# The first load of Q as two DMAs: 16 partitions and 112

## The chip, the cores and the metric

The kernel runs on one core of a Trainium2 chip. The metric is device microseconds of one execution, taken as the median of several runs. A profile is one more execution, recorded by the hardware profiler; it has a time of its own, and a span, which goes from the first to the last recorded instruction. A core has five instruction streams: PE (TensorE, matrix products; its weight loads are listed as PEld), DVE (VectorE), ACT (ScalarE), POOL (GpSimd) and SP (SyncE, which here only issues DMAs). Sixteen DMA engines move data between HBM and the core's on-chip memory, which has 128 partitions.

## What is computed

Linear attention over 8 batches of 12 heads, 512 positions of 64 features, all float32:

```python
Q_feat = np.maximum(0, Q) + 1
K_feat = np.maximum(0, K) + 1
KV = np.einsum('bhkd,bhkv->bhdv', K_feat, V)
K_sum = np.sum(K_feat, axis=2)
numerator = np.einsum('bhqd,bhdv->bhqv', Q_feat, KV)
denominator = np.einsum('bhqd,bhd->bhq', Q_feat, K_sum)
return (numerator / (denominator[:, :, :, None] + 1e-10)).astype(np.float32)
```

Each of Q, K, V and the output is 12.58 MB, so 50.33 MB pass between HBM and the core.

## The kernel before

The work is cut into 12 groups of 8 heads, and loads and stores cover 1 MB of the on-chip side as a rule. For a group g the stages are: `k_features` (DVE, K + 1 against 1, to bfloat16), `v_blocks` (V copied into a block layout, three quarters by DVE and one by ACT), `q_features` (DVE), `keys_values` (PE, the sums over positions, with ACT copying the result out), `transposes` (PE, with ACT copying), `out_matmuls` (PE) and `norms` (DVE, reciprocal and multiply). The main loop runs over the groups, with the output two groups behind and the stores three behind (`LAG`); the last two groups are written out by hand. The order on each engine is the order of the program.

Nearly all loads go through POOL's queue (`nc.gpsimd.dma_start`), which turns float32 in HBM into bfloat16 on the chip as it moves. They are `load` (line 115, K and V), `load_rest_q` (line 98) and `load_q` (line 121). Most stores go through POOL's queue too (line 135); those of the last two groups go through SP's (lines 138 and 141).

One load is different. `load_first_q` brings the first 128 x 2048 numbers of Q, one row of 8 KB for each partition, through SP's queue, and leaves them in float32 (line 93). It is the first thing that SP does. Beside it POOL issues, in this order: K and V of group 0, the second 128 rows of Q, K and V of group 1, and after some constants the loads of groups 2 and 3. The rows of `q_first` are read by DVE in `q_features` of groups 0 and 1 (line 146), after the features of K and the copies of V of group 0.

Of the kernel before, what the change touches and what calls it, by code (L numbers as in the profile page):

```python
# [19 lines left out]
def kernel(  # L20
# [19 lines left out]
    nc = tc.nc  # L40

    B, H, S, D = Q.shape
    P = 128
# [10 lines left out]
    def view(t, c):  # L54
        return t.flatten_outer_dims().rearrange("(n p c) d -> p n c d", p=P, c=c)

    q_eights = view(Q, C4)
# [32 lines left out]

    def load_first_q():
        t = head_pool.tile([P, C4, D], FP32, name="q_first")
        nc.sync.dma_start(out=t, in_=q_eights[:, 0])
        return t

    def load_rest_q(t):
# [159 lines left out]
    with tc.manual_schedule():  # L256
        nc.gpsimd.memset(zero, 0.0)
        q_first = load_first_q()
        load("k", (0,))
        load("v", (0,))  # L260
# [81 lines left out]
```

## Time and profile before

| | us |
|---|---|
| three runs, median (lowest to highest) | 126.62 (126.32 to 127.39) |
| the profiled execution | 126.47 |
| its span | 124.7 |
| DVE busy (share of the span) | 90.1 (72%) |
| PE busy | 64.2 (52%) |
| ACT busy | 59.6 (48%) |
| POOL busy | 26.1 (21%) |
| the first load of Q: issue to landing | 4.9 |
| the first loads of K and V: issue to landing | 7.0 and 8.7 |
| DVE's first read of the first load of Q starts at | 12.95 |

Times are counted from the start of the span. "L93" is line 93 of the kernel. A DMA is a set of packets, each handled by one of the sixteen DMA engines; a row of 8 KB of the first load is one packet. Queue q1 is SP's, q0 is POOL's, and q8 and q14 bring instructions. In a stretch of the span, the DMA share is the time of the packets that start in it, divided by sixteen engines and the stretch's length, so it can exceed 1 in a short stretch; GB/s counts bytes as they land, so a load that turns float32 into bfloat16 counts half of what it reads.

### The profile page before, as it was taken

What the parts mean: (1) busy time and instruction counts of PE and PEld (TensorE: products, weight loads), DVE (VectorE), ACT (ScalarE), POOL (GpSimd) and SP (SyncE); (2) the same over time, 40 slices, a digit from 0 to 9 for tenths busy, and PEclk for the clock granted to TensorE, in tenths of its full rate; (3) what the DMA queues carried; (4) which work ended last, traced back from release to release, by engine and by line L of the source; (5) the groups of instructions that cost most, each with busy time, mean ns of one, the idle gap of its engine ahead of it and who ended that gap; (6) DMA issues with size and microseconds to landing.
All of it is one profiled execution on the core that took longest, in us unless ns stands there. A gap on an engine that the chain in (4) does not pass through costs nothing.

```text
span 124.7 us, 2349 instructions
## 1 busy us (share of the span) xinstructions
PE 64.2 (52%) x960; PEld 52.6 (42%) x960; DVE 90.1 (72%) x190; ACT 59.6 (48%) x86; POOL 26.1 (21%) x53
## 2 busy tenths in 40 slices
PE   0000874600596837939099690069394369874200
PEld 0000654600475826829088490058183158663000
DVE  4875735206999989998999950799958799969700
ACT  7505169806009981398803981603982283650000
POOL 6992020400001460207202070302020200020000
PEclk9999999995559996799855999657999855999655
DMA  3999999999999999999999999999999999999993
GB/s 89 320 212 216 206 211 212 212 215 218 206 212 212 220 213 206 212 215 217 230 406 327 210 212 219 212 342 395 230 202 215 219 247 417 419 417 415 406 409 135
DMA packets 11819, 32.13 MB, mean 258 GB/s; under 512 B 544, under 2 KB 544, under 8 KB 11680
## 3 DMA queue, kind: packets, MB, share of 16 engines
q0 software_dynamic: 10592, 28.84, 97.5%
q1 hardware_dynamic: 1216, 3.15, 6.7%
q8 instruction: 7, 0.11, 0.3%
q14 instruction: 4, 0.03, 0.1%
HBM read 37.75 MB, written 12.58 MB: 404 GB/s over the span
## 4 chain that ended last, share of the span: by engine, by line
DMA 51%; DVE 19%; PE 10%; ACT 7%; POOL 6%; issue 2%; DVEq 0%; ACTq 0%; POOLq 0%
DMA v_raw<-in_V_dram 51%; DVE o_sb L232 7%; PE kva_ps L180 7%; DVE v_all L164 7%; ACT qt L204 3%; ACT v_all L162 3%; POOL kva_all L271 2%; POOL k_raw L115 2%; DVE recip L231 2%; PE qt_ps L201 1%; PE o_ps L214 1%; POOL v_raw L115 1%; DVE qf L146 1%; DVE qt L204 1%; DVE kf L146 1%
## 5 line engine op out<-in xcount | busy, mean ns | idle before, releaser
L180 PE MATMUL kva_ps<-v_all,kf 128*64 128x260 bf16 x384 | 33.0, 343 | 16.8 <-DVE v_all L164 15.5
L214 PE MATMUL o_ps<-kva_all,qt 128*64 128x130 bf16 x384 | 19.7, 237 | 34.2 <-DVE recip L231 25.9
L164 DVE COPY v_all<-v_raw 32x2048 bf16<-32x2048 bf16 x36 | 26.1, 725 | 15.0 <-DMA v_raw<-in_V_dram 14.6
L180 PEld LDWEIGHTS <-kf 128*64 128x64 bf16 x384 | 26.6, 140 | 20.4 <-DVE v_all L164 15.9
L232 DVE TENSOR_TENSOR o_sb<-o_ps,recip 128x512 f32<-128x512 f32 x48 | 33.2, 692 | 1.6
L162 ACT COPY v_all<-v_raw 32x2048 bf16<-32x2048 bf16 x12 | 22.6, 1893 | 18.2 <-DMA v_raw<-in_V_dram 18.0
L214 PEld LDWEIGHTS <-qt 128*64 128x64 bf16 x384 | 13.7, 116 | 39.1 <-issue 23.2
L190 ACT CAST kva_all<-kva_ps 64x256 bf16<-64x256 f32 x24 | 8.9, 370 | 30.7 <-PE kva_ps L180 30.6
L204 ACT COPY qt<-qt_ps 128x1024 bf16<-128x1024 bf16 x23 | 22.2, 1015 | 2.2 <-PE qt_ps L201 1.7
L201 PE MATMUL qt_ps<-identity,qf 128*128 128x128 bf16 x192 | 14.8, 236 | 1.3 <-ACT qt L204 1.1
L135 POOL DMA_DIRECT2D out_dram<-o_sb x10 | 8.3, 830 | 32.1 <-DVE o_sb L232 27.3
L146 DVE TENSOR_SCALAR kf<-k_raw 128x1024 bf16<-128x1024 bf16 x24 | 9.5, 436 | 7.0 <-DMA k_raw<-in_K_dram 7.0
L201 PEld LDWEIGHTS <-qf 128*128 128x128 bf16 x192 | 12.6, 107 | 4.1 <-issue 1.8
L115 POOL DMA_DIRECT2D k_raw<-in_K_dram x7 | 5.4, 765 | 34.4 <-DVE kf L146 34.0
L231 DVE RECIPROCAL recip<-o_ps 128x8 f32<-128x8 f32 x48 | 9.6, 200 | 1.5 <-PE o_ps L214 1.2
L115 POOL DMA_DIRECT2D v_raw<-in_V_dram x7 | 5.4, 772 | 17.4 <-ACT v_all L162 17.4
L146 DVE TENSOR_SCALAR qf<-q_raw 128x1024 bf16<-128x1024 bf16 x22 | 8.2, 432 | 0.0
L249 DVE MEMSET v_all<- 128x2600 f32 x2 | 4.5, 2225 | 1.1 <-issue 1.1
L191 ACT CAST kva_all<-kva_ps 64x4 bf16<-64x4 f32 x24 | 4.1, 169 | 0.0
L121 POOL DMA_DIRECT2D q_raw<-in_Q_dram x5 | 3.5, 705 | 0.0
L250 ACT COPY v_all<-zero 128x1560 f32<-128x1560 f32 x2 | 2.9, 1488 | 0.0
L271 POOL MEMSET kva_all<- 128x130 bf16 x16 | 2.4, 196 | 0.0
(14 smaller groups left out, 6.6 us busy)
## 6 DMA issues: line engine op xcount, KB each, us to landing
out_dram<-o_sb POOLq DMA_DIRECT2D x10, 1024.0 KB, 25.2
k_raw<-in_K_dram POOLq DMA_DIRECT2D x5, 1024.0 KB, 21.7
v_raw<-in_V_dram POOLq DMA_DIRECT2D x5, 1024.0 KB, 21.8
q_raw<-in_Q_dram POOLq DMA_DIRECT2D x5, 1024.0 KB, 25.9
q_first<-in_Q_dram SPq DMA_DIRECT2D x1, 1024.0 KB, 4.9
k_raw<-in_K_dram POOLq DMA_DIRECT2D x2, 512.0 KB, 9.7
v_raw<-in_V_dram POOLq DMA_DIRECT2D x2, 512.0 KB, 11.4
out_dram<-o_sb SPq DMA_DIRECT2D x1, 1024.0 KB, 7.0
```

The lines of the kernel that those rows point to most:

```text
L115: nc.gpsimd.dma_start(out=bufs[x, s][:, ms], in_=drams[x][:, of])
L135: nc.gpsimd.dma_start(out=o_to[:, g % 2 : 2 * NP : 2], in_=outs[s][:, g % 2 : 2 * NP : 2])
L146: nc.vector.tensor_scalar(out=dst, in0=src, scalar1=1.0, scalar2=1.0, op0=ALU.add, op1=ALU.max)
L162: nc.scalar.copy(out=v_all[ps, g % 2, :, :, b * D : b * D + D], in_=v_raw[ps])
L164: nc.vector.tensor_copy(out=v_all[ps, g % 2, :, :, b * D : b * D + D], in_=v_raw[ps])
L180: nc.tensor.matmul(kva_ps[64 * n : 64 * n + 64], lhsT=kf[:, c, n, :], rhs=v_all[:, g % 2, n, c, :], start=(c == 0), stop=(c == C2 - 1),)
L190: nc.scalar.copy(out=kva[ps, :, n, 0:D], in_=kva_ps[ps, 0 : 4 * D].rearrange("p (b d) -> p b d", b=4))
L201: nc.tensor.transpose(qt_ps[:, c, r], qf[:, r, 2 * half + c, :, :], identity)
L204: copy(out=qts[g // 2][:, lo : lo + 2], in_=qt_ps.rearrange("p c r q -> p c q r"))
L214: nc.tensor.matmul(ops[c // 4][64 * j : 64 * j + 64, c // 2 % 2, (c % 2) * W : (c % 2) * W + W], lhsT=qt[:, c, q : q + 16, :], rhs=kva[:, ...
L231: nc.vector.reciprocal(out=recip, in_=cells[:, :, :, :, D:D1])
L232: nc.vector.tensor_tensor(out=o_sb[:, 2 * h + g % 2 : 2 * NP : NP, 4 * i : 4 * i + 4].rearrange("p n (b c) d -> p b c n d", b=2), in0=cell ...
```

## The change

The one DMA of `load_first_q` becomes two of the same queue: the first brings partitions 0 to 15, the second partitions 16 to 127. The tile, its place and its later reads stay. DVE's first read of it now waits for both.

```diff
     def load_first_q():
         t = head_pool.tile([P, C4, D], FP32, name="q_first")
-        nc.sync.dma_start(out=t, in_=q_eights[:, 0])
+        nc.sync.dma_start(out=t[0:16], in_=q_eights[0:16, 0])
+        nc.sync.dma_start(out=t[16:P], in_=q_eights[16:P, 0])
         return t
```

On the engines the instructions keep their order; SP has one DMA more, ahead of its stores. Lines below 93 stand one lower in the changed kernel.

## The prediction

> **What bounds the kernel now.** I read the page's slices first, then its DMA queues, then stretches of the span at the start and the end, then the critical chain's place for SP's first load.
>
> The slices of the span (DMA is the mean busy share of 16 DMA engines in tenths) and the queue shares:
>
> ```profile
> DMA  3999999999999999999999999999999999999993
> ...
> q0 software_dynamic: 10592, 28.84, 97.5%
> q1 hardware_dynamic: 1216, 3.15, 6.7%
> q8 instruction: 7, 0.11, 0.3%
> ...
> HBM read 37.75 MB, written 12.58 MB: 404 GB/s over the span
> ```
>
> The DMA engines are full in every slice but the first and the last, while the busiest compute engine, DVE, works 72% of the span. So the time is: when the stream starts, plus bytes over rate, plus what follows the last byte. The change touches only the start. Busy times by stretch (columns: window, length, five engines' busy time with counts, TensorE clock, DMA share, GB/s):
>
> ```profile
> 1.00:1.70 0.70, 0.00 (x0) 0.00 (x0) 0.18 (x3) 0.70 (x1) 0.41 (x1) 1.00 0.00 0
> 1.70:1.90 0.20, 0.00 (x0) 0.00 (x0) 0.03 (x1) 0.20 (x1) 0.20 (x1) 1.00 2.84 328
> 1.90:2.50 0.60, 0.00 (x0) 0.00 (x0) 0.60 (x1) 0.59 (x2) 0.60 (x2) 1.00 0.00 0
> 2.50:2.90 0.40, 0.00 (x0) 0.00 (x0) 0.40 (x1) 0.40 (x1) 0.40 (x2) 1.00 0.51 205
> 2.90:4.90 2.00, 0.00 (x0) 0.00 (x0) 1.41 (x3) 2.00 (x2) 2.00 (x4) 1.00 1.04 434
> ...
> 121.80:123.50 1.70, 0.00 (x0) 0.00 (x0) 0.00 (x0) 0.00 (x0) 0.00 (x0) 0.50 0.51 195
> 123.50:124.70 1.20, 0.00 (x0) 0.00 (x0) 0.00 (x0) 0.00 (x0) 0.00 (x0) 0.50 0.00 0
> ```
>
> A packet counts in the stretch where it starts, with its whole duration. From 1.70 to 1.90 us start 328 GB/s x 0.2 us = 65.6 KB, that is 8 packets of 8 KB (one row of Q each); they take 2.84 x 16 x 0.2 / 8 = 1.14 us apiece. Then nothing starts for 0.6 us. From 2.50 on, 10 packets start in 0.4 us and take 0.51 x 16 x 0.4 / 10 = 0.33 us apiece, and from 2.90 on 434 x 2.0 / 8.192 = 106 packets, 0.31 us apiece. So eight of the sixteen engines begin at about 1.75 us with one slow packet, the other eight only at about 2.55, and both groups are in full stream by 2.9 to 3.1. At the end the engines stop one after the other between 121.8 and about 123.4: a share of 0.51 over 1.7 us is 0.87 us of work on the mean engine, so the mean engine ends near 122.7, and the last one, which sets the time, some 0.7 us later.
>
> What SP issues (start, duration, instruction):
>
> ```profile
> 0.74 0.39 SPq L93 DMA_DIRECT2D q_first<-in_Q_dram  x1
> 114.28 0.39 SPq L138 DMA_DIRECT2D out_dram<-o_sb  x1
> 115.96 2.05 SPq L141 DMA_DIRECT2D out_dram<-o_sb  x2
> ```
>
> **The change, part by part.** The profiled execution took 126.47 us, its span 124.7, so 1.77 us lie around the span; the sum is made against 126.47, which is 0.15 below the median 126.62 (126.32 to 127.39).
>
> *One issue more on SP.* One more L93 instruction, 0.39 us by its row. Behind it on SP stands only the store of L138, which goes out at 114.28, so the issue itself costs nothing. What it delays is the 112 rows: their issue runs from 1.13 to 1.52 instead of from 0.74. POOL's queue is not moved: its first K load is issued at 1.29 as before. DVE's first feature of Q now waits for two DMAs in place of one; it runs at 12.95, and Q landed at 0.74 + 4.9 = 5.6 us, 7.3 us of cover for DVE, for the queue behind that wait (the other features of Q, then K's and V's of group 1) and for TensorE's transposes. Without that cover the price would be the 0.39 us.
>
> *The start of the engines.* If the sixteen rows reach all sixteen engines at 1.75 and each streams at 0.31 us a packet from there, the late eight gain 2.55 - 1.75 = 0.8 us and the early eight lose their slow packet's excess, 1.14 - 0.31 = 0.83: a gain of 0.8 at most. The other end is no gain: the early eight hold a 0.8 us lead and have it eaten by the slow packet (1.75 + 1.14 = 2.89), while the late eight's first packets are over at 2.55 + 0.33 = 2.88. Both rows say that bytes begin to arrive at one moment, near 2.6 us, whoever asked first. I take -0.1: the nearest rows are these two, and they end together.
>
> *A second start.* At worst the 112 rows pay a slow first packet of their own: +0.83. But the late eight started 0.8 us after the early ones and their first packets took 0.33, so slowness belongs to the first request of all and not to each one; and the second issue is over 1.4 us before those first packets end. Below nothing cannot be: a second start removes no byte. I take 0. If an engine did find nothing of Q in between, the first K load (issued from 1.29 to 2.13) is the work that hides it; without it the hole is the 0.39 us between the issues.
>
> *Two completions.* One more 4-byte packet on each engine; the Q stretch shows 144 packets on this queue for 128 rows, so 16 closing packets ride on the load today without a gap that shows in the 434 GB/s. At most they cost a whole small packet's slot; I take 0.01.
>
> *Other shares of the rows.* Today each engine carries 8 rows of 8 KB. Evenly cut, it carries 1 and 7, and nothing is added; which partitions one engine writes at a time changes, and no row shows the price. From below it could gain what the stretch from 2.90 leaves: 106 packets at 0.314 against 0.309, so 0.04 us on eight packets. From above, three rows too many on an engine (the slower rival) are 3 x 0.31 = +0.93. I take +0.1, near the even cut.
>
> Sum: 0 - 0.1 + 0 + 0.01 + 0.1 = about 0. Against 126.47 that is 126.5; carried to the median of the runs (+0.15) 126.65. I write 126.7.
>
> [...] For the end of the program the trace has two SP stores of 0.5 MB back to back, both 6.4 us to landing, in an unbroken stream of 407 GB/s from 116.0 to 121.8; cutting a transfer made no hole and no speed there. [...]
>
> **The rivals.**
>
> *Faster: the whole 0.8 us.* All sixteen engines stream from 1.75. For it: eight engines do sit idle from 1.75 to 2.55. Against it: the slow 1.14 us packets of those that did not. Time 126.62 - 0.8 = 125.8. To pass 1% it would need 0.4 us more, which only a change in how the engines end could give. Chance 0.16, of which 0.07 past 1%.
>
> *Slower: uneven shares.* If the rows are dealt in blocks by partition (that only eight engines had work at 1.75 fits blocks: the first half of the partitions to eight engines), sixteen rows may fall on four engines, four rows each, and the 112 are then cut evenly: 4 + 7 = 11 rows instead of 8 on those four, +0.93 us there and -0.31 elsewhere. It decides as soon as one of the four is an engine that ends within 0.9 us of the last one; as the mean engine ends only 0.7 before the last, one of four nearly surely does. Time from +0.2 to +0.93: 126.8 to 127.55. Against it: 128 rows came out even. Chance 0.24; to pass 1% it must meet another loss, such as two of the seven instruction loads (0.3% of 16 x 124.7 us, so about 0.9 us each, each on one engine) coming together on one engine that had one before; 0.12 of the 0.24, with a little more for losses that I can't name.
>
> *It does nothing.* The hardware hands on both loads as one list and eight engines still begin at 2.55: 126.6. Chance 0.1.
>
> **How the numbers follow.** Forecast 0.5, nothing 0.1, faster 0.16, slower 0.24. I take 1% (1.27 us) as what a measurement of this kernel can tell from no change; the three runs shown lie 0.85% apart. So past 1% faster (below 125.35) 0.08, past 1% slower (above 127.9) 0.15, within 0.77. The range: from 125.6 (the full 0.8 with the 0.2 to 0.3 by which the lowest run lies under the median) to 127.8 (the 0.93 with the same spread above); that leaves some 2 in 10 outside, most of it above.
>
> **What would show it.** Right: from 1.70 to 1.90 us sixteen packets of 8 KB start instead of eight, each slow (about 1.1 us); the stretch from 2.9 to 4.9 stays at about 430 GB/s; V's first copy stays near 10.8 us and the last packets near 123.4. Faster is right if packets that start before 2.0 take 0.3 us and Q is over at 4.3 instead of 5.1. Uneven shares are right if fewer than sixteen packets start near 1.75 and the engines' ends spread over more than 1.7 us. The forecast is wrong if a hole appears in the DMA slices between 3 and 5 us, or if any stage past 10 us moves by more than the stream's start did.

## The result, and the profile after

| | before | changed |
|---|---|---|
| median (lowest to highest), 22 runs each | 126.67 us (126.32 to 127.46) | 127.18 us (126.73 to 127.91) |
| ratio, 95% interval | | 1.0034 (1.0019 to 1.0048) |
| the profiled execution, its span | 126.47, 124.7 us | 127.62, 125.8 us |

The change costs 0.34%, which is 0.43 us (0.24 to 0.61): within 1%, inside the range, but not nothing. (The two medians lie 0.51 us apart, inside that interval.) Single executions of one kernel spread over more than 1 us, so the 1.1 us between the two profiled spans must not be read as the price; the interval over many runs is the price.

The slices and the queues of the changed kernel's page, to be held against those of before:

```profile
DMA  3999999999999999999999999999999999999992
...
q0 software_dynamic: 10592, 28.84, 96.7%
q1 hardware_dynamic: 1232, 3.15, 7.3%
q8 instruction: 7, 0.11, 0.3%
...
HBM read 37.75 MB, written 12.58 MB: 400 GB/s over the span
```

The DMA engines still have no pause: every slice but the first and the last reads 9. SP's queue q1 has 16 packets more (the second DMA's closing packets: the trace has 80 packets of 4 bytes on this queue instead of 64) and the same 3.15 MB, but its packets took 7.3% of the engines' span instead of 6.7%: the same bytes went more slowly. The stretches of the start show where (columns as before: window, length, busy times, clock, DMA share, GB/s):

```profile
1.70:1.90 0.20, 0.00 (x0) 0.00 (x0) 0.03 (x1) 0.20 (x1) 0.20 (x1) 1.00 0.00 0
1.90:2.20 0.30, 0.00 (x0) 0.00 (x0) 0.30 (x1) 0.29 (x2) 0.30 (x2) 1.00 1.12 437
2.20:2.50 0.30, 0.00 (x0) 0.00 (x0) 0.30 (x1) 0.30 (x1) 0.30 (x1) 1.00 2.47 328
2.50:2.90 0.40, 0.00 (x0) 0.00 (x0) 0.40 (x1) 0.40 (x1) 0.40 (x2) 1.00 0.00 0
2.90:3.50 0.60, 0.00 (x0) 0.00 (x0) 0.60 (x1) 0.60 (x2) 0.60 (x2) 1.00 0.66 232
3.50:4.90 1.40, 0.00 (x0) 0.00 (x0) 0.81 (x3) 1.40 (x2) 1.40 (x3) 1.00 1.04 328
4.90:5.30 0.40, 0.00 (x0) 0.00 (x0) 0.40 (x1) 0.01 (x1) 0.32 (x2) 1.00 1.08 307
```

Worked as in the prediction: from 1.90 to 2.20 start 437 x 0.3 / 8.192 = 16 packets of 8 KB, the sixteen rows, at 1.12 x 16 x 0.3 / 16 = 0.34 us apiece: sixteen at once, one for each engine by estimate, none of them slow. From 2.20 on the first packets of the 112 rows follow, 12 of them at 2.47 x 16 x 0.3 / 12 = 0.99 us. Then comes the difference that matters: from 3.50 to 4.90 56 packets take 1.04 x 16 x 1.4 / 56 = 0.42 us apiece, and 0.46 from 4.90 to 5.30, where before the packets from 2.9 to 4.9 took 0.31 on the mean. The engines' share is full (1.04 and 1.08); each packet takes a third to a half longer.

SP's issues and DVE's first work on the loads in the changed kernel (start, duration, instruction, in brackets the idle time before it):

```profile
0.74 0.39 SPq L93 DMA_DIRECT2D q_first<-in_Q_dram  x1
1.19 0.41 SPq L94 DMA_DIRECT2D q_first<-in_Q_dram  x1
```

```profile
9.02 0.83 DVE L147 TENSOR_SCALAR kf<-k_raw 128x1024 bf16<-128x1024 bf16 x2 [1.16 <-DMA k_raw<-in_K_dram]
11.56 2.11 DVE L165 COPY v_all<-v_raw 32x2048 bf16<-32x2048 bf16 x3 [1.71 <-DMA v_raw<-in_V_dram]
13.71 0.69 DVE L147 TENSOR_SCALAR qf<-q_first 128x1024 bf16<-128x1024 f32 x1
```

and DVE's in the kernel before:

```profile
8.31 0.76 DVE L146 TENSOR_SCALAR kf<-k_raw 128x1024 bf16<-128x1024 bf16 x2 [0.46 <-DMA k_raw<-in_K_dram]
10.81 2.11 DVE L164 COPY v_all<-v_raw 32x2048 bf16<-32x2048 bf16 x3 [1.74 <-DMA v_raw<-in_V_dram]
```

K's first feature starts at 9.02 us against 8.31 before. K waits behind Q on the DMA engines: its load was issued at 1.29 us before and at 1.30 now, and no packet of POOL's queue starts until 4.9 and 5.7 us. So K shows how late the stream is: 0.71 us. DVE's read of Q itself, at 13.71, still waits for nothing.

### The profile page after: what moved, and what is told of

Its sections match the earlier page's. It is cut to its first block, busy times and chain, and to the rows that moved or that the text cites. A ratio compares the mean times of both kernels' runs of the same rounds, so it can differ in the third digit from the quotient of the medians.

```text
span 125.8 us, 2351 instructions
## 1 busy us (share of the span) xinstructions
PE 66.4 (53%) x960; PEld 54.7 (43%) x960; DVE 89.7 (71%) x190; ACT 59.6 (47%) x86; POOL 26.2 (21%) x53
## 3 DMA queue, kind: packets, MB, share of 16 engines
q1 hardware_dynamic: 1232, 3.15, 7.3%
## 4 chain that ended last, share of the span: by engine, by line
DMA 48%; DVE 23%; PE 11%; ACT 10%; issue 3%; POOL 1%; ACTq 0%; POOLq 0%
DMA v_raw<-in_V_dram 48%; DVE o_sb L233 9%; PE kva_ps L181 8%; DVE v_all L165 8%; ACT v_all L163 5%; ACT qt L205 3%; DVE qf L147 2%; DVE recip L232 2%; PE qt_ps L202 2%; ACT kva_all L191 2%; DVE kf L147 1%; DVE qt L205 1%; POOL k_raw L116 1%; PE o_ps L215 1%; ACT kva_all L192 0%
## 5 line engine op out<-in xcount | busy, mean ns | idle before, releaser
L181 PE MATMUL kva_ps<-v_all,kf 128*64 128x260 bf16 x384 | 32.5, 339 | 17.5 <-DVE v_all L165 16.0
L215 PE MATMUL o_ps<-kva_all,qt 128*64 128x130 bf16 x384 | 20.7, 247 | 32.9 <-DVE recip L232 21.7
L215 PEld LDWEIGHTS <-qt 128*64 128x64 bf16 x384 | 14.8, 123 | 38.0 <-issue 21.8
L202 PE MATMUL qt_ps<-identity,qf 128*128 128x128 bf16 x192 | 16.2, 248 | 0.9 <-ACT qt L205 0.6
L202 PEld LDWEIGHTS <-qf 128*128 128x128 bf16 x192 | 13.6, 113 | 3.7 <-issue 1.9
```

Of the source, the lines that this page charges most:

```text
L181: nc.tensor.matmul(kva_ps[64 * n : 64 * n + 64], lhsT=kf[:, c, n, :], rhs=v_all[:, g % 2, n, c, :], start=(c == 0), stop=(c == C2 - 1),)
L202: nc.tensor.transpose(qt_ps[:, c, r], qf[:, r, 2 * half + c, :, :], identity)
L215: nc.tensor.matmul(ops[c // 4][64 * j : 64 * j + 64, c // 2 % 2, (c % 2) * W : (c % 2) * W + W], lhsT=qt[:, c, q : q + 16, :], rhs=kva[:, ...
```

## The experiments

The theories at the first four runs:

- **A**: the loss lies in where a DMA writes. Rows that go to neighbouring partitions at one time get in each other's way, the sixteen rows above all. (A "write path" below is my guess at a way into the memory that several partitions share; no run shows such a path by itself.)
- **B**: every second DMA pays a start of its own.
- **C**: the loss lies in the cut of the 112 rows, seven to an engine.

**Sixteen rows ahead of the whole, to neighbouring partitions and spread.** Both kernels keep Q's load in one DMA and send sixteen rows to a spare tile before it:

```diff
+        u = head_pool.tile([P, C4, D], FP32, name="spare")
+        nc.sync.dma_start(out=u[0:16], in_=q_eights[0:16, 0])
         nc.sync.dma_start(out=t, in_=q_eights[:, 0])
```

In the other one the first of the two DMAs writes `u[0:P:8]`, every eighth partition.

> Q's first load is one DMA of 128 rows as before, but ahead of it on SP's queue the first sixteen rows also go to partitions 0 to 15 of a spare tile that nobody reads. That adds 131 KB, 0.31 us of the stream at 424 GB/s. Theory A (sixteen neighbouring partitions take writes slowly: in the changed kernel that DMA's last packets started by 2.5 us but it landed at 3.84): it lands about 3.1 us after its issue again, the first packets behind it take 0.9 to 1.3 us, the later ones of the 128 rows 0.31 us as before, and K's first feature, at 8.31 before, starts at 9.1 to 9.3. Theory B (any second DMA pays a start of its own, 0.4 to 0.8 us): also 9.0 to 9.4. Theory C (the loss sits in the cut of the 112 rows, seven to an engine): only the bytes count, 8.6 to 8.7, and packets of 0.31 us throughout.

> As the run before, the same sixteen rows of HBM ahead of Q's 128, but into every eighth partition of the spare tile. Theory A: the crowd is gone or halved, the small DMA lands about 2.2 to 2.6 us after its issue instead of 3.1, and K's first feature starts at 8.6 to 8.8, at least 0.3 us before the run with neighbouring partitions. Theory B: no difference from that run, 9.0 to 9.4. Theory C: 8.6 to 8.7 in both.

With neighbouring partitions K's first feature started at 8.53, in line with the added bytes alone (8.31 + 0.31 = 8.62). The first packets of the 128 rows, from 2.20 on, took 3.30 x 16 x 0.3 / 16 = 0.99 us apiece, but from 2.90 to 4.90 us the packets took 0.86 x 16 x 2.0 / 86 = 0.32:

```profile
2.20:2.50 0.30, 0.00 (x0) 0.00 (x0) 0.30 (x1) 0.30 (x1) 0.30 (x1) 1.00 3.30 437
2.90:4.90 2.00, 0.00 (x0) 0.00 (x0) 1.41 (x3) 2.00 (x2) 2.00 (x4) 1.00 0.86 352
```

So behind sixteen rows in neighbouring partitions and a second start the 128 rows go on at their full pace (0.32 us a packet, 0.31 before). A had the slow first packets right (0.9 to 1.3 us) but not K's start (9.1 to 9.3), which B missed too (9.0 to 9.4); C had K's start nearly (8.6 to 8.7), but not the slow first packets. Time 1.0032 (1.0006 to 1.0058).

Spread over the partitions, the sixteen rows were worse, not better: K's feature at 9.22 and 1.0099 (1.0065 to 1.0132, four runs). No theory had expected it. SP's issues took 0.57 and 0.56 us there instead of 0.38 and 0.41, and the first packets started 0.3 us later, at 2.08 instead of 1.75. Q itself landed 0.5 us later (1.36 + 5.1 against 1.18 + 4.8); where the rest of K's 0.69 us went is open. The landing of the sixteen rows says something else. With neighbouring partitions, then spread:

```profile
spare<-in_Q_dram SPq DMA_DIRECT2D x1, 128.0 KB, 2.7
spare<-in_Q_dram SPq DMA_DIRECT2D x1, 128.0 KB, 2.6
```

From their first packet to their landing they took 0.74 + 2.7 - 1.75 = 1.7 us in neighbouring partitions and 0.74 + 2.6 - 2.08 = 1.3 us when spread. This is the one pair of runs in which only the partitions differ.

**The same shares cut by columns.** All 128 partitions twice, first 1 KB of each row and then 7 KB:

```diff
-        nc.sync.dma_start(out=t, in_=q_eights[:, 0])
+        nc.sync.dma_start(out=t[:, 0:4], in_=q_eights[:, 0, 0:4])
+        nc.sync.dma_start(out=t[:, 4:C4], in_=q_eights[:, 0, 4:C4])
```

> Q's first load as two DMAs of all 128 partitions: the first 1 KB of each row, then the other 7 KB; the same bytes in the same shares as the changed kernel, every engine with the rows it has today. Theory A: no loss from where the rows go; Q lands at 5.6 to 5.9 us, K's first feature at 8.3 to 8.5, time 126.5 to 126.9. Theory B: a second start, K's first feature at 8.8 to 9.1 and 127.0 to 127.4. Theory C: as A, since no row count changes.

K's first feature at 8.51, 0.2 later, within what A and C had said (8.3 to 8.5) but for 0.01; B's 8.8 to 9.1 did not come. The time was 1.0042 (1.0023 to 1.0061), more than 0.2 us would give: here B's number was the better one. From 2.90 to 4.90 us 373 x 2.0 / 7.168 = 104 packets of 7 KB took 0.92 x 16 x 2.0 / 104 = 0.28 us apiece, near seven eighths of 0.31, so at full pace:

```profile
2.90:4.90 2.00, 0.00 (x0) 0.00 (x0) 1.41 (x3) 2.00 (x2) 2.00 (x4) 1.00 0.92 373
```

A second DMA with next to no bytes, below, takes up what B has left.

**Halves.**

```diff
-        nc.sync.dma_start(out=t, in_=q_eights[:, 0])
+        nc.sync.dma_start(out=t[0:64], in_=q_eights[0:64, 0])
+        nc.sync.dma_start(out=t[64:P], in_=q_eights[64:P, 0])
```

> Q's first load as two DMAs of 64 partitions each, 0 to 63 and 64 to 127. Theory A, in the form that each write path serves a few neighbouring partitions and a DMA of half of the partitions has half of the paths: each half moves at half pace, the 8 KB packets take about 0.6 us instead of 0.31, Q lands at 7.5 to 8 us, and K's first feature starts at 10 to 10.7; time 127.5 to 129. Theory B: one more start as with 16 and 112, K's first feature at 8.8 to 9.1, time about 127.1. Theory C (seven rows to an engine is the odd cut): four rows each is even, 8.3 to 8.5 and 126.7.

A in the form above had it: K's first feature at 10.37, time 1.0131 (1.0098 to 1.0164). The stretch from 2.90 to 4.90 us:

```profile
2.90:4.90 2.00, 0.00 (x0) 0.00 (x0) 1.41 (x3) 2.00 (x2) 2.00 (x4) 1.00 1.04 232
```

The engines are full (1.04) and move 232 GB/s, where one DMA of 128 rows moved 434: 0.58 us a packet, near the 0.6 of A. That half of the partitions means half of the paths is A's reading; the run shows the half pace.

**The other order.**

```diff
-        nc.sync.dma_start(out=t, in_=q_eights[:, 0])
+        nc.sync.dma_start(out=t[16:P], in_=q_eights[16:P, 0])
+        nc.sync.dma_start(out=t[0:16], in_=q_eights[0:16, 0])
```

> The two DMAs of the changed kernel in the other order: partitions 16 to 127 first, then 0 to 15. After the first four runs theory C reads: the 112 rows, seven neighbouring partitions to an engine, take 0.4 to 0.5 us a packet instead of 0.31, in whatever place they stand, because engines then write the same part of the memory at the same time. By it the 8 KB packets of the 112 rows again take 0.4 us or more from 3 us on, K's first feature starts at 8.9 to 9.2 (9.02 in the changed kernel, 8.31 before), and the time is 0.2 to 0.6% over before. Theory A (the sixteen rows ahead do it): packets of 0.31 us, K's first feature at 8.3 to 8.5.

```profile
2.90:4.90 2.00, 0.00 (x0) 0.00 (x0) 1.41 (x3) 2.00 (x2) 2.00 (x4) 1.00 1.08 352
```

Packets of 1.08 x 16 x 2.0 / 86 = 0.40 us, K's first feature at 9.10, time 1.0029 (0.9999 to 1.0059, which just takes in no loss). It isn't what goes first; the 112 rows are slow (0.40 us, where the 128 took 0.31) without sixteen ahead of them.

**A second DMA without bytes, and no change at all.**

```diff
         nc.sync.dma_start(out=t, in_=q_eights[:, 0])
+        u = head_pool.tile([P, 1, D], FP32, name="spare")
+        nc.sync.dma_start(out=u[0:16], in_=q_eights[0:16, 0, 0:1])
```

> Q's first load as before in one DMA; behind it on SP's queue a second one of 16 x 256 B into a spare tile that nobody reads. It adds a second DMA and no bytes worth counting. If a second DMA costs time by itself, however it starts (the column cut delayed K by only 0.2 us and yet measured 0.42% over before), this is 0.2 to 0.4% over before as well. If only shape and bytes count: K's first feature at 8.3 to 8.4 and a ratio of 1.000 within its interval.

> The kernel before, unchanged, measured against itself as every other kernel here is: what difference this comparison shows where there is none. Every theory expects a ratio of 1.000 within its interval; if it lies 0.2% or more from it, differences of 0.3% here say little.

```profile
8.18 0.89 DVE L148 TENSOR_SCALAR kf<-k_raw 128x1024 bf16<-128x1024 bf16 x2 [0.32 <-DMA k_raw<-in_K_dram]
8.14 0.92 DVE L146 TENSOR_SCALAR kf<-k_raw 128x1024 bf16<-128x1024 bf16 x2 [0.29 <-DMA k_raw<-in_K_dram]
```

The second DMA alone: K's first feature at 8.18, time 0.9989 (0.9955 to 1.0022). The unchanged kernel: 8.14 and 0.9985 (0.9949 to 1.0020). They can't be told apart, so a second issue on SP and its closing packets cost nothing that shows, and B falls in the form that any second DMA costs. It doesn't fall for a DMA that starts behind a short one: there the first packets were slow (0.99 us), and what the column cut lost is not explained. The control also says that a ratio's interval here is some 0.35% to either side, and that K's start moves by 0.2 us from one execution to the next.

**Two queues.**

```diff
-        nc.sync.dma_start(out=t, in_=q_eights[:, 0])
+        nc.sync.dma_start(out=t[0:64], in_=q_eights[0:64, 0])
+        nc.scalar.dma_start(out=t[64:P], in_=q_eights[64:P, 0])
```

> The halves of Q's first load from two queues at once, partitions 0 to 63 from SP's and 64 to 127 from ACT's. One after the other they moved at half pace (packets of 0.6 us, K's first feature at 10.37). If that pace belongs to which partitions are written at one time, the two halves side by side fill all of it: Q lands at 5.2 to 6 us, K's first feature starts at 8.2 to 8.7 and the time is 126.2 to 126.8. If it belongs to the cut of each DMA (four rows to an engine), packets stay near 0.6 us and K's first feature is near 10.

K's first feature at 9.80, time 1.0070 (1.0042 to 1.0097). That is what the cut of each DMA would give, but it decides little, since the halves did not run side by side. The two issues were out together at 0.74 us; SP's half landed 4.8 us later and ACT's 7.1:

```profile
q_first<-in_Q_dram ACTq DMA_DIRECT2D x1, 512.0 KB, 7.1
q_first<-in_Q_dram SPq DMA_DIRECT2D x1, 512.0 KB, 4.8
```

**Eight DMAs of sixteen rows**, in neighbouring partitions and in every eighth. The number of DMAs, and of rows in each, is the same in both:

```diff
-        nc.sync.dma_start(out=t, in_=q_eights[:, 0])
+        for p in range(0, P, 16):
+            nc.sync.dma_start(out=t[p : p + 16], in_=q_eights[p : p + 16, 0])
```

```diff
-        nc.sync.dma_start(out=t, in_=q_eights[:, 0])
+        for p in range(8):
+            nc.sync.dma_start(out=t[p:P:8], in_=q_eights[p:P:8, 0])
```

> Q's first load as eight DMAs of sixteen neighbouring partitions each, one row to an engine. [...] That sentence aside, the changed kernel's sixteen rows had their last packet started by 2.2 us and landed at 3.84, over 1 us late, so I take 1.0 to 1.2 us for each of the eight: 8 to 9.6 us, Q landed at 10 to 12, K's first feature at 13 to 15.5 where it was 8.31, and 130 to 134 us in all. Theory C' (only the number of rows that an engine has in a DMA, or the number of DMAs, counts): SP issues one in 0.41 to 0.57 us, eight in 3.3 to 4.6, so the last is out by 4 to 5.3 us, Q has landed by 6 to 7, K's first feature is at 8.5 to 9.5, and the time is below 128.

> As the run before, eight DMAs of sixteen rows with one row to an engine, but the rows of one DMA are every eighth of the 128, in partition and in HBM. [...] Theory C': as the run before within 0.5 us, since the number of DMAs and of rows is the same.

In neighbouring partitions the time fell where A had it (130 to 134): 130.63 us, 1.0298 (1.0242 to 1.0353). Spread it was 128.69 us, 1.0144 (1.0096 to 1.0191), 1.9 us less, where C' had the two within 0.5. Spreading the same eight DMAs halves the loss, 3.8 us to 1.8, although SP's eight issues took longer there (5.24 us in all against 3.63). Other marks missed. Q's last DMA landed at 3.96 + 10.2 = 14.2 us in neighbouring partitions, where A had 10 to 12 and C' 6 to 7, and at 5.38 + 7.0 = 12.4 us when spread, where C' had the same within 0.5. K's first feature was the wrong mark: it started at 9.59 and 8.13, since K landed before Q's last rows. What stands behind all of Q's rows shows it, V's first copy (10.81 before). In neighbouring partitions:

```profile
14.48 2.12 DVE L165 COPY v_all<-v_raw 32x2048 bf16<-32x2048 bf16 x3 [3.93 <-DMA v_raw<-in_V_dram]
```

and spread:

```profile
12.59 2.11 DVE L165 COPY v_all<-v_raw 32x2048 bf16<-32x2048 bf16 x3 [3.51 <-DMA v_raw<-in_V_dram]
```

3.7 us late and 1.8 us late, with DVE waiting for the load in both. The stream shows how: in 2 to 4, 8 to 10, 10 to 12 and 12 to 14 us the DMA share of the kernel with neighbouring partitions is 0.93 to 1.47, full, at 132 to 167 GB/s:

```profile
2.00:4.00 2.00, 0.00 (x0) 0.00 (x0) 2.00 (x1) 1.99 (x3) 2.00 (x4) 1.00 0.93 137
...
8.00:10.00 2.00, 0.00 (x0) 0.00 (x0) 0.41 (x1) 0.00 (x0) 1.98 (x3) 1.00 1.47 163
10.00:12.00 2.00, 0.00 (x0) 0.00 (x0) 0.55 (x2) 0.00 (x0) 0.00 (x0) 1.00 1.05 132
12.00:14.00 2.00, 0.00 (x0) 0.00 (x0) 0.00 (x0) 0.00 (x0) 0.00 (x0) 1.00 1.45 167
```

From 10 to 12 us the spread kernel moves 210 GB/s at a share that is no higher:

```profile
10.00:12.00 2.00, 0.00 (x0) 0.00 (x0) 0.00 (x0) 0.00 (x0) 0.09 (x1) 1.00 1.04 210
```

**The change once more.** The changed kernel itself.

> The changed kernel once more, for a second profile of its start and a second measurement. If what the first profile shows belongs to the kernel: K's first feature at 8.9 to 9.1, packets of 0.4 to 0.5 us from 3.5 to 5.7 us, and a ratio of 1.002 to 1.006. If the start of 9.02 was one execution's: a K start nearer 8.5.

```profile
3.50:4.90 1.40, 0.00 (x0) 0.00 (x0) 0.81 (x3) 1.40 (x2) 1.40 (x3) 1.00 1.04 322
```

K's first feature at 9.09, packets of 1.04 x 16 x 1.4 / 55 = 0.42 us from 3.5 to 4.9, ratio 1.0032 (1.0007 to 1.0056). The start belongs to the kernel, not to one execution.

## Why the prediction was right, and where not

*The number held, the signs did not.* The measured 127.18 us lies 0.48 above the 126.7 that was written, inside the range. But of the signs named for being right, three failed. Sixteen packets did start at once, but fast ones (0.34 us, not about 1.1). The stretch from 2.9 to 4.9 us fell from 434 GB/s to 299:

```profile
2.90:4.90 2.00, 0.00 (x0) 0.00 (x0) 1.41 (x3) 2.00 (x2) 2.00 (x4) 1.00 0.93 299
```

And V's first copy moved from 10.81 to 11.56. So the start of the stream went otherwise than forecast, and that the number came out near is in part luck: two wrong terms cancelled, and a third, too small, reached the end only in part.

*Right: what bounds, and what is covered.* The time is the DMA stream's: no slice between the first and the last reads under 9, and with eight DMAs V's first copy was 3.7 and 1.8 us late and the time 3.8 and 1.8 us longer. SP's second issue (0.41 us) and the second closing packets cost nothing that shows: the second DMA without bytes measured 0.9989, the unchanged kernel 0.9985. DVE's wait for two DMAs was covered; its read of Q came at 13.71, with Q landed at 1.19 + 5.8 = 6.99.

*Right by size, by luck: no gain at the start.* The term was -0.1 us, on the ground that bytes begin to arrive at one moment near 2.6 us whoever asks first. They don't: in the changed kernel sixteen packets that started from 1.90 took 0.34 us apiece and were done by 2.5. Sixteen packets did start at once, as the faster rival had it, and the lead was lost in what followed.

*Wrong, and hidden by the term above: the second start.* I took slowness to belong to the first request of all and put 0. In the changed kernel the first packets of the second DMA were slow, 0.99 us instead of 0.31, close to the worst case of +0.83 that I had weighed and put aside. It ate the lead of at most 0.8. The run with sixteen rows ahead of all 128 shows the two together: its first packets behind the sixteen rows took 0.99 us as well, and K was late by the added bytes alone. Why these packets are slow was not settled. Nor are eight early and eight late engines a fixed trait of the one DMA, as I had read them: in the control's profile of the unchanged kernel six packets started from 1.70 to 1.90 (246 x 0.2 / 8.192), and eleven more before 2.5, at 0.62 x 16 x 0.6 / 11 = 0.54 us:

```profile
1.70:1.90 0.20, 0.00 (x0) 0.00 (x0) 0.04 (x1) 0.20 (x1) 0.20 (x1) 1.00 2.08 246
1.90:2.50 0.60, 0.00 (x0) 0.00 (x0) 0.60 (x1) 0.59 (x2) 0.60 (x2) 1.00 0.62 150
```

*Mis-sized: the other shares of the rows.* This is the term that failed most. I put +0.1 us for "which partitions one engine writes at a time changes", near a cut into one and seven rows to an engine that was my estimate and that no run had shown, and kept +0.93 only for three rows too many on an engine. What the changed kernel showed in its place: the sixteen rows went out as sixteen packets at once (1.90 to 2.20 us, 0.34 us apiece), not four to an engine one after the other, so the slower rival fell, yet the packets of the 112 rows took 0.42 to 0.46 us instead of 0.31, with 0.40 in the other order and 0.42 in the repeat. For the six packets that each engine has left after its first slow one that is 6 x 0.11 to 6 x 0.15 = 0.7 to 0.9 us by estimate, and K started 0.71 us later than before, 0.88 later than in the control's profile (9.02 - 8.14). The 128 rows kept 0.32 us behind sixteen others.

*Why these packets are slower is argued, not shown.* The runs speak for the partitions that are written together. With the same number of DMAs, and of rows in each, eight spread DMAs lost half of what eight neighbouring ones did (1.8 us to 3.8), though with them the order of the rows in HBM changed too. Halves ran at 232 instead of 434 GB/s, though each DMA had 64 rows, four to an engine by estimate instead of eight. The sixteen rows ahead, of which only the partitions changed, landed 1.3 instead of 1.7 us after their first packet, though that kernel as a whole was slower. That the same thing slows seven neighbouring rows to an engine is an inference: no run changed only the partitions of the 112 rows.

*Open: from 0.71 us to 0.43.* The stream starts 0.7 to 0.9 us late and the time grows by 0.24 to 0.61, in the repeat by 0.09 to 0.71. Part of the delay does not reach the end in the median, while in the columns run 0.2 us at the start went with 0.29 to 0.77 at the end (1.0023 to 1.0061 of 126.49). That run and the one with sixteen neighbouring rows ahead (1.0032, with 0.31 us of added bytes) had packets at full pace and yet lost as much as the changed kernel. So the slow packets account for the late stream at the start; that they account for the 0.34% of the whole is not shown. The engines stop one after another over 1.7 us (121.8 to 123.5 in the kernel before, at a share of 0.51), and single executions scatter by more than the differences. These runs don't settle it.

*The price of a cut by partitions.* My sum had it at about nothing. The runs give it a price: halves cost 1.3% (1.0131), sixteen and 112 cost 0.3% (1.0034).

## What to carry to other kernels

Before a load is cut by partitions, ask which partitions are written at the same time: the one DMA over all 128 had its packets at 0.31 us after the first ones, and each cut by partitions that was tried slowed the packets (0.40 to 0.58 us in three kernels) or delayed the stream (V's first copy 1.8 us late with eight spread DMAs). In this program, whose DMA engines never rest, the idle start that was saved came to nothing: the packets behind it took 0.99 and then 0.42 us. So compare packet durations (share x engines x window / packets) and not busy shares, which read full in both cases (1.04 and 1.04). A mark for lateness must stand behind the whole of what was changed: K's start told the truth for two DMAs and misled for eight (9.59, with V's first copy 3.7 us late).

## What the runs showed that was not expected

- Two loads issued at the same moment on SP's and ACT's queues did not run side by side: one half landed at 5.5 us, the other at 7.8 (ACT's issue at 0.74 with 7.1 to landing).
- With eight DMAs the engines went over to POOL's queue before this load was through, although SP had issued all of it by 4.4 us in neighbouring partitions: from 3.80 to 6.60 no row of this load started there, and K's first feature came at 9.59 with Q's last DMA landing at 14.2. Why was not settled.
- SP's issue of one DMA took 0.38 to 0.42 us for most loads, but 0.55 to 0.58 for the halves and 0.56 to 0.57 where sixteen rows went to every eighth partition, for the load behind them too; the first packets then started near 2.1 us instead of 1.75 to 1.96.
- Sixteen rows spread over the partitions ahead of the whole load cost more (0.99%) than the same rows in neighbouring partitions (0.32%).
